# Two score products of 256 columns a head, with a query's two parts in the partition halves, in place of three of 512 a head pair

## The chip, the cores and the metric

The kernel runs on one core of a Trainium2 chip. The metric is the time of one execution on the device in microseconds. The core has five engines with a queue each: TensorE (PE in the profile; its weight loads are PEld), VectorE (DVE), ScalarE (ACT), GpSimd (POOL) and SyncE (SP), which issues the loads from memory. They work in parallel and wait for one another through semaphores.

## The reference

One decoder layer over 512 tokens of width 1024, all in 32-bit floats: a gated feed-forward half step (1024 to 2 x 2816 and back), a token mixer, a second feed-forward half step, and a gated embedding at the end. The mixer's attention is the part that is changed:

```python
s = jnp.einsum('bnqhgd,bnkhd->bnhgqk', qb, kb) * scale     # 16 query heads, 2 key heads, 64 wide
valid = (delta >= 0) & (delta < WINDOW) & (kpos >= 0)      # window of 128: this block and the one before
s = jnp.where(valid, s, NEG_INF)
m = jnp.maximum(jnp.max(s, -1, keepdims=True), sink)
pr = jnp.exp(s - m)
denom = jnp.sum(pr, -1, keepdims=True) + jnp.exp(sink - m)
o = jnp.einsum('bnhgqk,bnkhd->bnqhgd', pr / denom, vb)
```

Beside the attention the mixer has a branch with a causal convolution of 31 taps over 1024 channels and a layer norm, and two gates; the sum of both branches goes through one more matrix.

## The kernel before, in words

**Products in two parts.** Activations lie feature by token, in tiles of 128 features x 512 tokens. A 32-bit value is split into a high part, rounded to a shorter type that TensorE takes as it is (F32R), and a low part, the rest in the same type. ScalarE writes the high part, VectorE subtracts it from the value to get the low one (`split_into`). A product of two values is then three products on TensorE (`mm3`): low by high, high by high, high by low; low by low is left out. Every weight piece of 128 x 1024 is loaded, split and used so, through three buffers each for the raw piece, its high and its low part. In the list of weights, those of the mixer may be split on VectorE or on GpSimd (`FLEX`).

**The scores.** The 16 query heads lie in two groups g of eight, and the tokens in four blocks t of 128. `scores(g, t)` (L1083) takes four head pairs. Four transposes bring the queries of the block from token-major `zq` to `qTp`, in which a pair j stands with one head in partitions 0 to 63 and the other in 64 to 127. These two heads belong to the two different key heads. The keys `kz` (L1024) hold, for each key head, the 64 features in that head's half of the partitions and zeros in the other half; four memsets on GpSimd write the zeros. So a product of a pair's 128 partitions with the keys of both heads side by side gives each head's own scores: 2 x 256 columns where two key blocks are seen, 2 x 128 for t = 0, which sees one. With the three products of `mm3` that is 12 products for a call. ScalarE and VectorE then take the scores from PSUM under the mask, and VectorE takes maxima. `softmax` and `values` follow as separate steps.

**What sets the order.** The kernel is written as a list of operations, and a planner on the host puts them in order. The string `ORDER` (L40) names the steps of the mixer in the order in which TensorE should take them: K keys and values, Q queries, a and b the two projections of the convolution, A scores, E softmax, V values, g and h gates, p the attention's projection, L the norm of the convolution, e the embedding. `simulate` runs the list against costs from a table (`costs`, L291; a load is priced by its bytes over a rate, L344): each engine takes its ready operation with the earliest due time, TensorE takes groups of products from the next eight of the list, and operations of `nc.flex` go to whichever of VectorE and GpSimd comes first. Five rounds are made with due times from the round before, and the best one is kept. The program issues the operations in that order, and on the chip each engine keeps to it. So a new cost or a new step order moves operations on all engines.

**Names.** `q0b`, `q1b` are the query projections of the two groups, `kvb` that of keys and values, `ca`, `cb` those of the convolution, `ga`, `gb` gates, `ap` the attention's projection, `cp` the convolution's, `wo` the mixer's last one; `sc` scores, `pT` transposed probabilities and `p` their parts, `po` a masked copy of these, `o` values, `of` their sum, `oT` its parts; `cz` the running sum of a convolution channel in PSUM (VectorE, one operation a tap), `ct` taps of the channels that ScalarE and GpSimd do, `ln_` the convolution's norm, `cv` its result's parts, `e` and `ple` the embedding.

Of the kernel before, what the change touches and what calls it, by code (L numbers as in the profile page):

```python
# [9 lines left out]
F32 = mybir.dt.float32  # L10
F32R = mybir.dt.float32r
I32 = mybir.dt.int32
AF = mybir.ActivationFunctionType
# [3 lines left out]
P = 128  # L17
# [8 lines left out]
HD = 64  # L26
# [11 lines left out]


ORDER = """  # L40
K0 a0 a2 a1 Q0 A0 b2 b1 b0 a3 A1 E0 E1 b3 A2 E2 a4 V0 A3 a5 E3 V1 b4 Q1 V2 b5
A4 V3 A5 a7 A6 g5 h7 E5 A7 E6 E4 V6 g3 E7 g0 a6 V5 V4 g4 g6 b6 V7 h1 g2 h4 b7
g1 p0 p2 g7 L0 p3 p6 p4 h3 p7 p5 p1 e0 h5 h6 e1 h0 h2
"""
POOLCH = (0, 2, 4)
WARM = 9
# [178 lines left out]
class Program:  # L225
# [65 lines left out]
    def costs(self, op, eng=None):  # L291

        ins = op.reads
        o = op.writes[0] if op.writes else None
        n = max([v.free() for v in ([o] if o else []) + ins])
        psum = any(v.vt.cls == "ps" for v in op.writes + ins)
        eng = eng or op.eng
        op.lock = eng == "POOL"
        op.fset = None
        op.dma = 0.0  # L300
        vecs = sum(isinstance(v, V) for v in [*op.a[3:], *(v for n, v in op.k.items() if n != "accum_out")])
        if eng == "PE":
            if op.what == "transpose":
                op.cost, op.lat = 0.112, 0.3
            else:
                n = op.a[2].free()
                if op.a[2].vt.dtype == F32R:
                    op.cost, op.lat = (0.2275, 0.3) if n > 256 else (0.121, 0.3)
                else:
                    op.cost, op.lat = max(0.15, n * 0.00167), 0.35  # L310
        elif eng == "DVE":
            op.lat = 0.15
            if op.what == "tensor_tensor":
                op.cost = 0.065 + n * 1.055e-3
            elif op.what == "scalar_tensor_tensor":
                op.cost = 0.08 + n * 1.12e-3
            elif op.what == "tensor_tensor_reduce":
                op.cost = 0.28 + n * 1.02e-3
            elif op.what in ("reduce_sum", "tensor_reduce"):
                op.cost = 0.08 + n * 1.03e-3  # L320
            else:
                op.cost = 0.08 + n * (1.25e-3 if psum else 0.9e-3)
            op.lock = not psum and op.what not in ("tensor_tensor_reduce", "reduce_sum", "tensor_reduce", "reciprocal")
        elif op.what == "dma_start" and eng == "ACT":
            op.cost, op.lat = 0.5, 2.6
        elif eng == "ACT":
            op.cost, op.lat = 0.07 + n * 0.88e-3, 0.17
            op.cost += 0.094 * vecs
            if "accum_out" in op.k:
                op.cost += 0.1  # L330
            f = op.a[2].name if len(op.a) > 2 else "Copy"
            op.fset = SETS.get(f)
        elif eng == "POOL":
            op.lat = 0.15
            if op.what == "tensor_tensor":
                op.cost = 0.14 + n * 2.1e-3
            elif op.what == "tensor_scalar":
                op.cost = 0.25 + n * 0.8e-3
            else:
                op.cost = 0.12 + n * 1.0e-3  # L340
        else:
            op.cost, op.lat = 0.47, 0.0
            v = (op.writes + op.reads)[0]
            op.dma = v.free() * v.shape[0] * 4 / 360e3  # L344


class Engine:
# [296 lines left out]
def record():  # L644
# [8 lines left out]
    def rtile(name):  # L653
        return nc.tile(name, [P, S], F32R, "a")
# [367 lines left out]


    kz = [nc.tile(f"kz{p}", [P, NKV, S], F32R, "k") for p in "hl"]  # L1024
    for z in kz:
        nc.gpsimd.memset(z.bitcast(F32)[HD:P, 0], 0.0)
        nc.gpsimd.memset(z.bitcast(F32)[0:HD, 1], 0.0)


    vd = [nc.tile(f"v{t}", [P, 2, NKV, 2, HD], F32R, "a") for t in range(NT)]  # L1030
# [3 lines left out]
    def keys_values():  # L1034
# [26 lines left out]
        halves = [slice(hh * HD, (hh + 1) * HD) for hh in range(2)]  # L1061
        for hh in range(2):
            r = halves[hh]
            split_into(kz[0][r, hh], kz[1][r, hh], pt[r])

    zq, rq = {}, {}

# [15 lines left out]
    def scores(g, t):  # L1083
# [6 lines left out]
        with nc.group(f"qT{g}_{t}"):  # L1090
            for j in range(4):
                nc.tensor.transpose(pt[:, j * P : (j + 1) * P], zq[g, t][:, j * P : (j + 1) * P], ident)
        qT = split(f"qT{g}_{t}", pt)
        nb = 1 if t == 0 else 2
        t0 = t + 1 - nb
        s = [nc.tile(f"s{g}_{t}_{i}", [P, 2, 2, W], F32, "a") for i in range(2)]
# [1 line left out]
        for j in range(4):  # L1098
            ps = ps_tile(f"sc{g}_{t}_{j}")
            ps4 = ps.rearrange("p (h c k) -> p h c k", h=2, c=2)  # L1100
            with nc.group(f"sc{g}_{t}_{j}"):
                q = [qT[i][:, j * P : (j + 1) * P] for i in range(2)]
                kk = [kz[i][:, :, t0 * W : (t + 1) * W] for i in range(2)]
                mm3(ps4[:, :, 0:nb], q, kk, True, True)
            sj = s[j // 2][:, j % 2]
            if t == 0:
                nc.vector.tensor_tensor(sj, ps4[:, :, 0], later, op=ALU.add)
            else:
                nc.scalar.copy(sj, ps4[:, :, 1])
                nc.vector.copy_predicated(sj, later.bitcast(I32), ps4[:, :, 0])  # L1110
            if j % 2:
                mj = m[:, 2 * j - 2 : 2 * j + 2].rearrange("p (j h) -> p j h", h=2)
                nc.vector.tensor_reduce(mj, s[j // 2], axis=AX.X, op=ALU.max, negate=True)
# [332 lines left out]
```

## Time and profile before

| | |
|---|---|
| median of 3 runs | 1203.24 us (1203.09 to 1203.4) |
| the profiled execution, its span | 1205.14 us, 1203.4 us |
| TensorE busy | 1193.8 us, 99% |
| VectorE busy | 729.6 us, 61% |
| ScalarE busy | 506.7 us, 42% |
| GpSimd busy | 319.4 us, 27% |
| granted clock of TensorE | 0.999 |
| first feed-forward step, mixer, second step, embedding gate | to 369, to 803, to 1152, to 1203.4 us |

A time of a run is the device's; the span is that between the first and the last instruction of one execution that was taken with the profiler. A row of a group gives the line, the engine, the operation, out<-in with the shapes and the count, then busy time in us and the mean time of one in ns, then the idle time of the engine ahead of them. A row of the chain of waits or of the timeline gives start and length in us. A row of windows gives the stretch, its length, the busy time of an engine with its number of operations, the granted clock, the share of the DMA engines and GB/s. Nearly all operations are issued at one line of the kernel (L1346; L1354 in the changed file), so they are told apart by their tiles.

### The profile page before, as it was taken

The page shows a single profiled execution, that of the slowest core. Times are in us where ns is not written, and L with a number is a line of the kernel's source. Part 1 is how long each engine was busy: PE and PEld are TensorE (multiplying, and loading weights), DVE is VectorE, ACT ScalarE, POOL GpSimd, SP SyncE. Part 2 cuts the span into 40 slices and gives each one's busy share as a digit, 9 for nine tenths or more (in the row PEclk, how much of TensorE's full clock was granted, in tenths as well). Part 3 has the DMA queues.
Part 4 walks back from the last instruction along what each step waited for, and adds up shares of the span by engine and source line. Part 5 has one row for each costly group of instructions (what it writes and reads, how often), then busy time and mean ns, then how long its engine had stood idle before and what let it go on. Part 6 is the DMA issues. An engine that isn't in the chain of part 4 may idle for free.

```text
span 1203.4 us, 14206 instructions
## 1 busy us (share of the span) xinstructions
PE 1193.8 (99%) x5380; PEld 990.4 (82%) x5380; DVE 729.6 (61%) x1034; ACT 506.7 (42%) x821; POOL 319.4 (27%) x340
## 2 busy tenths in 40 slices
PE   9999999999999999999999999999999999999997
PEld 7888888888888888878888888888888888888886
DVE  5644444444444799998898786665444444444455
ACT  6423232332223669879854673323323332222232
POOL 1000000001111887887897500430000000011110
PEclk9999999999999999999999999999999999999999
DMA  7322223233332321212233222323232323333321
GB/s 222 105 92 100 96 98 100 88 114 97 97 101 88 105 88 53 89 53 71 76 101 101 92 88 89 104 88 105 88 105 88 105 90 99 96 97 96 101 88 71
DMA packets 36069, 115.06 MB, mean 96 GB/s; under 512 B 4512, under 2 KB 7200, under 8 KB 36000
## 3 DMA queue, kind: packets, MB, share of 16 engines
q1 hardware_dynamic: 35856, 114.12, 29.5%
q8 instruction: 42, 0.69, 0.2%
q14 instruction: 27, 0.22, 0.1%
q10 hardware_dynamic: 144, 0.03, 0.0%
HBM read 112.04 MB, written 2.10 MB: 95 GB/s over the span
## 4 chain that ended last, share of the span: by engine, by line
PE 96%; DVE 3%; issue 0%; ACT 0%; DMA 0%; POOL 0%; DVEq 0%; ACTq 0%; POOLq 0%
PE f_g L1346 20%; PE f_u L1346 20%; PE f_d L1346 20%; PE gb L1346 4%; PE cb L1346 4%; PE pg L1346 4%; PE wo L1346 4%; PE ap L1346 4%; PE cp L1346 4%; PE ca L1346 3%; PE ga L1346 3%; PE q0b L1346 2%; PE sc L1346 1%; DVE cz L1346 1%; PE kvb L1346 1%; PE e L1346 1%
## 5 line engine op out<-in xcount | busy, mean ns | idle before, releaser
L1346 ACT ACTIVATE whi_wgu<-raw_wgu 128x1024 fp32r<-128x1024 f32 (+1 forms) x100 | 95.1, 956 | 254.4 <-PE f_u L1346 231.1
L1346 DVE TENSOR_TENSOR wlo_wgu<-raw_wgu,whi_wgu 128x1024 fp32r<-128x1024 f32 (+1 forms) x100 | 110.8, 1112 | 112.0 <-ACT whi_wgu L1346 111.1
L1346 DVE TENSOR_TENSOR wlo_wd<-raw_wd,whi_wd 128x1024 fp32r<-128x1024 f32 (+1 forms) x48 | 65.8, 1370 | 101.9 <-ACT whi_wd L1346 101.9
L1346 ACT ACTIVATE whi_wd<-raw_wd 128x1024 fp32r<-128x1024 f32 (+1 forms) x48 | 47.5, 990 | 174.6 <-PE f_d L1346 113.1
L1346 POOL TENSOR_TENSOR y<-y,ct 128x509 f32<-128x509 f32 (+28 forms) x90 | 114.9, 1297 | 6.8 <-ACT ct L1346 5.1
L1346 DVE SCALAR_TENSOR_TENSOR cz<-u,dww,cz 128x504 f32<-128x504 f32 (+26 forms) x145 | 103.9, 731 | 1.7
L1346 POOL TENSOR_TENSOR pg_ss_sq<-x 128x512 f32<-128x512 f32 x8 | 8.3, 1041 | 338.1 <-DVE x L1346 324.1
L1346 POOL TENSOR_TENSOR mix_ss_sq<-x 128x512 f32<-128x512 f32 x8 | 8.3, 1041 | 328.3 <-DVE x L1346 316.3
L1346 DVE TENSOR_TENSOR f_gs<-f_g,f_n_rb 128x512 f32<-128x512 f32 x44 | 30.3, 691 | 94.4 <-PE f_g L1346 93.0
L1346 PE MATMUL f_d<-f_a_h,wlo_wd 128*128 128x512 f32 x224 | 87.1, 389 | 0.0
L1346 PE MATMUL f_d<-f_a_h,whi_wd 128*128 128x512 f32 x224 | 87.1, 389 | 0.0
L1346 PE MATMUL f_d<-f_a_l,whi_wd 128*128 128x512 f32 x224 | 87.1, 389 | 0.0
L1346 PE MATMUL f_g<-h_h,whi_wgu 128*128 128x512 f32 x176 | 69.1, 393 | 0.6 <-ACT whi_wgu L1346 0.6
L1346 PE MATMUL f_g<-h_h,wlo_wgu 128*128 128x512 f32 x176 | 69.2, 393 | 0.0
L1346 PE MATMUL f_g<-h_l,whi_wgu 128*128 128x512 f32 x176 | 69.0, 392 | 0.0
L1346 PE MATMUL f_u<-h_h,wlo_wgu 128*128 128x512 f32 x176 | 68.8, 391 | 0.0
L1346 PE MATMUL f_u<-h_l,whi_wgu 128*128 128x512 f32 x176 | 68.7, 390 | 0.0
L1346 PE MATMUL f_u<-h_h,whi_wgu 128*128 128x512 f32 x176 | 68.7, 390 | 0.0
L1346 PE MATMUL f_g<-f_h_h,wlo_wgu 128*128 128x512 f32 x176 | 68.6, 390 | 0.0
L1346 PE MATMUL f_g<-f_h_l,whi_wgu 128*128 128x512 f32 x176 | 68.5, 389 | 0.0
L1346 PE MATMUL f_u<-f_h_h,wlo_wgu 128*128 128x512 f32 x176 | 68.5, 389 | 0.0
L1346 PE MATMUL f_g<-f_h_h,whi_wgu 128*128 128x512 f32 x176 | 68.5, 389 | 0.0
(402 smaller groups left out, 3144.0 us busy)
## 6 DMA issues: line engine op xcount, KB each, us to landing
raw_wgu<-in_wgu SPq DMA_DIRECT2D x84, 512.0 KB, 3.5
raw_wd<-in_wd SPq DMA_DIRECT2D x32, 512.0 KB, 3.5
raw_wzc<-in_wzc SPq DMA_DIRECT2D x16, 512.0 KB, 3.4
raw_wzg<-in_wzg SPq DMA_DIRECT2D x16, 512.0 KB, 3.5
raw_wd<-in_wd SPq DMA_DIRECT2D x16, 384.0 KB, 3.1
raw_wq<-in_wq SPq DMA_DIRECT2D x8, 512.0 KB, 3.5
raw_wap<-in_wap SPq DMA_DIRECT2D x8, 512.0 KB, 3.5
raw_wcp<-in_wcp SPq DMA_DIRECT2D x8, 512.0 KB, 3.5
```

Source lines behind the costliest of these rows:

```text
L1346: getattr(engines[op.eng], op.what)(*a, **k)
```

## The change

The two parts of a query go into the two halves of the partitions. For each of the two heads of all pairs there is a tile `qT[hh]`: the high part stays in the half where the head came out of the transposes, and the low part is written into the other half. The keys of a head stand in both halves, in the high tile and in the low tile, so there are no zeros and no memsets. One product of `qT[hh]` with a key part then sums the high and the low query part against that key part; two products, with the low and with the high keys, make the scores of one head, low by low included. A call has 16 products, of 256 columns each, or of 128 for t = 0, where it had 12 of 512, or of 256. The splits are two on ScalarE and two on VectorE for a call, each on 64 partitions, where there was one of each on 128; for the keys there are four of each where there were two. With it come a new `ORDER`, and in the planner a load's rate of 240e3 in place of 360e3 bytes a microsecond.

```diff
 ORDER = """
-K0 a0 a2 a1 Q0 A0 b2 b1 b0 a3 A1 E0 E1 b3 A2 E2 a4 V0 A3 a5 E3 V1 b4 Q1 V2 b5
-A4 V3 A5 a7 A6 g5 h7 E5 A7 E6 E4 V6 g3 E7 g0 a6 V5 V4 g4 g6 b6 V7 h1 g2 h4 b7
-g1 p0 p2 g7 L0 p3 p6 p4 h3 p7 p5 p1 e0 h5 h6 e1 h0 h2
+K0 a0 a1 b1 Q0 b0 a2 b2 A0 a3 A1 b3 A2 E0 a4 V0 E1 A3 a5 E2 V1 b4 E3 Q1 V3 b5
+A4 g5 A5 a6 E4 A6 E5 V2 a7 b7 A7 g3 V5 b6 E6 h4 g4 V6 E7 g2 V4 V7 g6 g1 e0 g0
+p0 L0 p5 h2 h5 h3 h1 p6 p4 p3 p2 h6 e1 h7 h0 g7 p7 p1
 """
...
-            op.dma = v.free() * v.shape[0] * 4 / 360e3
+            op.dma = v.free() * v.shape[0] * 4 / 240e3
...
     kz = [nc.tile(f"kz{p}", [P, NKV, S], F32R, "k") for p in "hl"]
-    for z in kz:
-        nc.gpsimd.memset(z.bitcast(F32)[HD:P, 0], 0.0)
-        nc.gpsimd.memset(z.bitcast(F32)[0:HD, 1], 0.0)
...
             r = halves[hh]
-            split_into(kz[0][r, hh], kz[1][r, hh], pt[r])
+            for to in (r, halves[1 - hh]):
+                nc.scalar.activation(kz[0][to, hh], pt[r], AF.Copy)
+            for to in (r, halves[1 - hh]):
+                nc.vector.tensor_tensor(kz[1][to, hh], pt[r], kz[0][r, hh].bitcast(F32), op=ALU.subtract)
...
-        qT = split(f"qT{g}_{t}", pt)
+        qT = [rtile(f"qT{g}_{t}_{hh}") for hh in range(2)]
+        for hh in range(2):
+            r, other = (slice(h * HD, (h + 1) * HD) for h in (hh, 1 - hh))
+            nc.scalar.activation(qT[hh][r], pt[r], AF.Copy)
+            nc.vector.tensor_tensor(qT[hh][other], pt[r], qT[hh][r].bitcast(F32), op=ALU.subtract)
...
-                q = [qT[i][:, j * P : (j + 1) * P] for i in range(2)]
-                kk = [kz[i][:, :, t0 * W : (t + 1) * W] for i in range(2)]
-                mm3(ps4[:, :, 0:nb], q, kk, True, True)
+                for hh in range(2):
+                    for i in (1, 0):
+                        nc.tensor.matmul(
+                            ps[:, 2 * hh * W : (2 * hh + nb) * W], qT[hh][:, j * P : (j + 1) * P],
+                            kz[i][:, hh, t0 * W : (t + 1) * W], start=i == 1, stop=i == 0,
+                        )
```

The order moves as follows at three places. The first is TensorE at the first scores of the second query group (block t = 0). Before, from the transposes of the queries on (the 22 rows left out are the rest of the projection ca):

```order
L1346 MATMUL pT_3_0_4135<-ident,s_3_1_3728 128x128 x2
L1346 MATMUL qTp_0_4142<-ident,zq_0_4089 128x128 x4
L1346 MATMUL pT_3_1_4150<-ident,s_3_0_3697 128x128 x2
L1346 MATMUL pT_3_1_4150<-ident,s_3_1_3728 128x128 x2
L1346 MATMUL qTp_1_4160<-ident,zq_1_4096 128x128 x4
L1346 MATMUL ca_4170<-mix_h_h,wlo_wzc_4024 128x512
...
L1346 MATMUL sc_0_0_4228<-kzh,qT_0_l 128x2x128
L1346 MATMUL sc_0_0_4228<-kzh,qT_0_h 128x2x128
L1346 MATMUL sc_0_0_4228<-kzl,qT_0_h 128x2x128
```

The same place in the change:

```order
L1354 MATMUL qTp_0_4200<-ident,zq_0_4099 128x128 x4
L1354 MATMUL o_3_0_4208<-p_3_0_h,v_2773 128x512
L1354 MATMUL o_3_0_4208<-p_3_0_l,v_2773 128x512
L1354 MATMUL o_3_0_4208<-po_3_0h,v_2781 128x512
L1354 MATMUL o_3_0_4208<-po_3_0l,v_2781 128x512
L1354 MATMUL o_3_1_4219<-p_3_1_h,v_2773 128x512
L1354 MATMUL o_3_1_4219<-p_3_1_l,v_2773 128x512
L1354 MATMUL o_3_1_4219<-po_3_1h,v_2781 128x512
L1354 MATMUL o_3_1_4219<-po_3_1l,v_2781 128x512
L1354 MATMUL qTp_1_4229<-ident,zq_1_4108 128x128 x4
L1354 MATMUL sc_0_0_4239<-kzl,qT_0_0_4216 128x128
L1354 MATMUL sc_0_0_4239<-kzh,qT_0_0_4216 128x128
```

The projection ca no longer stands between the transposes and the scores; two groups of value products of the first head group do, and the transposes of the next block.

The second is VectorE at the same place, in the change. The operations qT are those that write the low query parts, of those that sum the values:

```order
L1354 TENSOR_TENSOR wlo_wzc_4183<-raw_wzc_4005,whi_wzc_4167 128x1024
L1354 SCALAR_TENSOR_TENSOR cz_3981<-u_3965,dww,cz_3981 128x500
L1354 SCALAR_TENSOR_TENSOR cz_3981<-u_3965,dww,cz_3981 128x499
L1354 TENSOR_TENSOR sga_4212<-ga_4140,mix_n_rb 128x512
L1354 SCALAR_TENSOR_TENSOR cz_3981<-u_3965,dww,cz_3981 128x498
L1354 TENSOR_TENSOR qT_0_0_4216<-qTp_0_4200,qT_0_0_4216 64x512
L1354 TENSOR_TENSOR qT_0_1_4224<-qTp_0_4200,qT_0_1_4224 64x512
L1354 TENSOR_TENSOR of_3_4231<-o_3_0_4208,of_3_4231 64x512
L1354 TENSOR_TENSOR of_3_4231<-o_3_1_4219,of_3_4231 64x512
L1354 TENSOR_TENSOR qT_1_0_4241<-qTp_1_4229,qT_1_0_4241 64x512
L1354 TENSOR_TENSOR qT_1_1_4249<-qTp_1_4229,qT_1_1_4249 64x512
```

Each block has two such operations where it had one, and they stand behind a weight split, tap operations and a gate of the projection ga.

The third is TensorE from the spread of the convolution norm's factors to the first convolution projection, in the change (rows left out are the rest of the two projections ap):

```order
L1354 MATMUL ln_v_sp<-ln_v_dgl,ones_r 128x512
L1354 MATMUL ap_6026<-oT0h,wlo_wap_5906 128x512
...
L1354 MATMUL ple_sp<-ple_dgh,ones_r 128x512
L1354 MATMUL ple_sp<-ple_dgl,ones_r 128x512
L1354 MATMUL ap_6078<-oT0h,wlo_wap_5943 128x512
...
L1354 MATMUL cp_6130<-cv_h,wlo_wcp_6036 128x512
```

Before, three quarters of the last embedding projection e and two gates gb stood there; now it is two projections ap.

## The prediction

> **What bounds the kernel now.** I read the page first, then TensorE's waits, then the windows by stage, then single groups.
>
> ```profile
> span 1203.4 us, 14206 instructions
> PE 1193.8 (99%) x5380; PEld 990.4 (82%) x5380; DVE 729.6 (61%) x1034; ACT 506.7 (42%) x821; POOL 319.4 (27%) x340
> PE 96%; DVE 3%; issue 0%; ACT 0%; DMA 0%; POOL 0%; DVEq 0%; ACTq 0%; POOLq 0%
> 249.34 119.68 PE f_d L1346 x528
> ```
>
> The first two rows are the page's head and its busy times, the third the chain that ended last by engine, the fourth one piece of that chain. TensorE is busy for all but 9.6 us of the span, and carries 96% of the chain. The fourth row gives the price that everything below uses: 528 products of 512 columns follow one another in 119.68 us, 0.2267 us from start to start (the 389 ns that the groups show for one is its latency, not its price). What else keeps the PE idle is little:
>
> ```profile
> PE warm L1346 <- DVE ones L1346: 1.1, 1, 1.1
> PE ca L1346 <- DVE of L1346: 1.1, 1, 1.1
> PE f_g L1346 <- ACT whi_wgu L1346: 0.6, 1, 0.6
> PE sc L1346 <- DVE of L1346: 0.3, 1, 0.3
> ```
>
> These four rows are all of its waits: 1.7 us at the start, which the change has no part in, and 1.4 us in the token mixer. So time is won only by giving TensorE less to do, and lost by making it wait. The engine that could make it wait is VectorE, in the stretch where the scores lie:
>
> ```profile
> 410.00:432.00 22.00, 20.83 (x25) 1.00 0.30 95
> 432.00:450.00 18.00, 17.93 (x42) 1.00 0.26 88
> 450.00:487.00 37.00, 35.13 (x67) 1.00 0.18 59
> 487.00:527.00 40.00, 38.71 (x61) 1.00 0.24 80
> 527.00:563.00 36.00, 33.72 (x67) 1.00 0.18 59
> 563.00:600.00 37.00, 31.75 (x46) 1.00 0.22 72
> 600.00:630.00 30.00, 28.54 (x40) 1.00 0.32 104
> 630.00:663.00 33.00, 28.02 (x38) 1.00 0.30 98
> ```
>
> Each row is a stretch, its length, and VectorE's busy time in it. From 410 to 663 us it is busy 234.6 of 253 us: 18.4 us are free, but only 4.4 of them before 527 us.
>
> **The scores of blocks t = 1 to 3.** Six of the eight calls have two key blocks.
>
> ```profile
> 442.73 1.43 PE sc L1346 x12
> 458.72 2.72 PE sc L1346 x12
> 369.02 11.51 PE kvb L1346 x96
> L1346 PE MATMUL sc<-kzh,qT_l 128*128 128x512 f32 x24 | 9.5, 397 | 0.3 <-DVE of L1346 0.3
> L1346 PE MATMUL kvb<-whi_wkv,mix_h_l 128*128 128x256 f32 x32 | 9.1, 283 | 0.0
> L1346 PEld LDWEIGHTS kvb<-whi_wkv,mix_h_l 128*128 128x128 f32 x32 | 6.1, 192 | 0.0
> ```
>
> Rows one to three are pieces of the chain: a t = 0 call, a later call, and the key and value projection. Now a later call is 12 products of 512, 2.72 us; 24 of each of three kinds, 72 x 0.2267 = 16.32 us. After the change it is 16 products of 256, 96 in all. That operation is in the trace: the key and value projection is 96 products of 256 columns, of the same type, each with a stationary tile of its own, in 11.51 us, 0.1199 each, although a weight load is shown as 192 ns; the loads overlap. So 96 x 0.1199 = 11.51 us, and this part saves 16.32 - 11.51 = **4.81 us**. The stationary tile now serves two products in a row; I count no gain for that, since two of each old triple share one too, and the t = 0 call still pays 1.43 / 12 = 0.119 for each.
>
> **The scores of block t = 0.** Two calls of 12 products of 256 columns, 2 x 1.43 = 2.86 us, become 32 products of 128 columns. The trace has no product of this type under 256 columns, so it is bounded.
>
> ```profile
> 467.21 1.03 PE L1346 MATMUL pT<-ident,s 128*128 128x128 f32 x8
> 468.00 0.47 PE L1346 MATMUL sc<-kzh,qT_l 128*128 128x512 f32 x1
> L1346 PE MATMUL warm<-ones 128*128 128x128 f32 x18 | 4.2, 430 | 1.1 <-DVE ones L1346 1.1
> 8.00 1.28 PE f_u L1346 x3
> ```
>
> The first two rows are single instructions in order of time, the third a group, the fourth a piece of the chain at the start. From below: 256 columns less cost 0.2267 - 0.1199 = 0.1068 us, so 128 less would cost 0.0534, leaving 0.0665 us each, 2.13 us, 0.73 less than now. From the nearest row: eight transposes of 128 columns, each with a new stationary tile, take from 467.21 to 468.00, 0.099 each: 32 x 0.099 = 3.17 us, 0.31 more than now. From above: the plain 32-bit warm-up products of 128 columns show 18 instructions for 9 calls in 4.2 us, 0.467 a call, at a time when three 512-column products took 1.28 us instead of 0.68; in the steady state that is 0.467 x 0.68 / 1.28 = 0.248 a call, and 32 x 0.248 = 7.94 us, 5.08 more than now. I take the transposes, as they have the same sizes: **+0.31**, from -0.73 to +5.08. This is the part in which narrower products speak against the change.
>
> By the Trainium skill (TensorE: Matmul & The Clock Gate, section LDWEIGHTS) a weight load takes its number of columns over 1.2, in ns, about 107 ns for 128 columns, whatever the matmul behind it. A product shorter than that would be held by its load, and the sum of this block would be 32 x 0.107 = 3.4 us, about 0.55 more than now. The 0.099 us of the transposes agrees to a tenth; no row here shows it for this type.
>
> **ScalarE and VectorE.** The operations change from one of 128 partitions to two of 64.
>
> ```profile
> L1346 ACT ACTIVATE kzh<-kTp x2: 577/588/598, 410.7 to 411.3; 64x512 fp32r<-64x512 f32 x2
> L1346 DVE TENSOR_TENSOR kzl<-kTp,kzh x2: 676/686/695, 411.9 to 412.6; 64x512 fp32r<-64x512 f32 x2
> L1346 ACT ACTIVATE qT_h<-qTp x8: 573/594/616, 437.8 to 541.2; 128x512 fp32r<-128x512 f32 x8
> L1346 DVE TENSOR_TENSOR qT_l<-qTp,qT_h x8: 676/683/692, 438.8 to 541.8; 128x512 fp32r<-128x512 f32 x8
> L1346 DVE TENSOR_TENSOR wlo_wgu<-raw_wgu,whi_wgu 128x1024 fp32r<-128x1024 f32 (+1 forms) x100 | 110.8, 1112 | 112.0 <-ACT whi_wgu L1346 111.1
> 487.00:527.00 40.00, 19.15 (x28) 1.00 0.24 80
> ```
>
> The first four are forms of one tile with their shortest, middle and longest time in ns; the fifth is a weight split; the last is the window from 487 to 527 us for the tap operations cz alone. Half the partitions cost the same (686 against 683 ns, 588 against 594). So eight query splits and two key splits more on each engine: VectorE gains 8 x 0.68 + 2 x 0.69 = 6.8 us, ScalarE 8 x 0.59 + 2 x 0.59 = 5.9 us. In the new order GpSimd also does two weight splits fewer (14, not 16), which VectorE then does at 1.11 us each: 9.0 us in all. GpSimd loses its four memsets, which lie at the start beside other work. ScalarE is at 42% and I price it at nothing beyond the chain below. VectorE's 9.0 us fit into its 18.4 free ones; the cover is the long row of tap operations cz, which nobody waits for before the norm of the convolution. Without that cover it would be those 9.0 us.
>
> **Where the new order is narrow.** At the first call of the second head group the old order had a whole projection (24 products, 5.44 us) between the transposes qTp_0 and the products. The new one has two value groups and four transposes: 8 x 0.2267 + 4 x 0.099 = 2.2 us. In that time ScalarE must do two halves and VectorE two, of which the last sub must follow the last copy: 0.59 + 0.59 + 0.68 = 1.9 us and the handovers between. Behind the two halves on VectorE stand the subtractions of_3 that free the value banks, so a late one there is late twice. I charge 0.5 us, up to 3 if VectorE comes to it late. On the other side the old stall (PE ca, 1.1 us, and sc, 0.3) stood just where this order is rewritten: after the query projection q1b there now stands a whole ga projection before the next transposes. It may go: -1.4.
>
> The second place is the convolution's norm.
>
> ```profile
> 688.09 0.39 PE L1346 MATMUL ln_v_sp<-ln_v_dgl,ones_r 128*128 128x512 f32 x1
> 689.18 0.60 ACT L1346 COPY ln_v_rb<-ln_v_sp 128x512 f32<-128x512 f32 x1
> 690.97 1.28 ACT L1346 ACT_TABLE_LOAD   x1
> 700.48 0.81 ACT L1346 ACTIVATE y<-y,g_all 128x512 f32<-128x512 f32 x1
> 701.70 0.82 ACT L1346 ACTIVATE y<-y,g_all 128x512 f32<-128x512 f32 x1
> 704.23 0.39 PE L1346 MATMUL cp<-cv_h,wlo_wcp 128*128 128x512 f32 x1
> ```
>
> Now cp follows ln_v_sp by 16 us; in the new order two ap projections and ple_sp lie between, 2 x 5.44 + 0.45 = 11.3 us. ScalarE needs from ln_v_sp 1.3 us to the end of the copy, 0.5 for a gate, 1.28 for the table, 8 x 1.22 (the step from one y to the next, 700.48 to 701.70), 1.5 for a copy and a weight split put in between; VectorE's last sub adds 0.7: 15.1 us. The eighth channel is wanted at 11.3 + 7 x 0.68 = 16.1. It holds by 1 us, and I charge nothing. Over both places and the old stall I take **+0.3**, from -1.4 to +3.
>
> The planner's dearer DMAs move some small loads and two splits of p ahead; weights still come through three buffers that TensorE frees, so I price it at zero, within 0.3 either way.
>
> **The sum.** -4.81 + 0.31 + 0.3 = -4.2 us. The profiled execution took 1205.14 us around its span of 1203.4; it becomes 1200.9, and the median of the runs shown, 1203.24, becomes **1199.0**. With the bounds of the likeliest case (t = 0 at 0.0665 to 0.12 a product, stalls -1.4 to +1.5) it lies from 1196.3 to 1200.9.
>
> **Rivals.**
>
> *Under 256 columns this type falls back to the price of the plain one.* Then t = 0 costs +5.08, and the time is 1203.24 - 4.81 + 5.08 + 0.3 = 1203.8. For it: the warm-up rows show that the plain type pays double instructions. Against it: nothing here shows the type switching. The Trainium skill (FP8 and Floating Point Precision, section TensorE Precision Notes) says that true FP32 takes four passes through the array; by that t = 0 would cost about four times its columns, much like the rows' bound.
>
> *New waits eat most of it*: 3 us at the two narrow places, 1203.24 - 4.81 + 0.31 + 3 = 1201.7. For it: VectorE has 1.3 us free from 487 to 527. Against it: 19.15 of its 38.71 us there are cz, which can wait.
>
> *VectorE becomes the bound (slower).* If its free time is not free but the waiting of an ordered queue, its added 9.0 us come out at ln_mb, which waits for the last cz, and everything behind it is late by 9.0 us less what can be filled. With a third of the 18.4 us filled, 9.0 - 6.1 = 2.9 us: 1206.1. It means slower than before by over 0.2% from the point at which less than 6.6 us can be filled. Against it: TensorE waits for VectorE 1.4 us today with VectorE 97% busy, and in the new order the work that stands ahead of ln_mb on TensorE is, by the prices above, 1.4 us more than now.
>
> *The change gives nothing because loads bind*: at 188 to 192 ns a load, 128 products would take 24 us instead of 19.2: 1208. The key and value row above all but excludes it.
>
> **Chances.** Likeliest 62%, fall-back to the plain price 14%, new waits 14%, VectorE the bound 8%, loads 2%. The runs tell a change from none at about 0.2%, 2.4 us, so 1200.8 and 1205.6 are the borders. The likeliest case lies under 1200.8 almost whole, and a little of the waits with it: faster 0.64. The fall-back and nearly all of the waits lie between: same 0.27. Slower 0.09. The range reaches from 1196.8 over the waits to the fall-back, 1204.
>
> **What would show it.** The sc groups: x48 of 256 columns for each key part, and a later call's piece of the chain at 1.92 us instead of 2.72; a t = 0 call at 1.6 (right), 1.1 (lower bound) or 4 (fall-back). VectorE's busy time near 738.6 us. TensorE's waits should still sum to about 3 to 4 us; a wait of sc or o on VectorE at the second head group, or of cp on cv, is the second rival, and one of ln_mb on ln_s_l the third. A wrong price of 256 columns, or stalls that grow by over 2 us, would make the prediction wrong.

## The result and the profile after

| | before | after |
|---|---|---|
| median of 5 runs | 1203.36 us (1203.09 to 1205.06) | 1211.07 us (1210.1 to 1215.47) |
| ratio to before, 95% interval | | 1.0063 (1.0052 to 1.0073) |
| the profiled execution, its span | 1205.14 us, 1203.4 us | 1211.07 us, 1209.4 us |

The change was to save 4.2 us and costs 7.7 by the medians. Executions of one kernel start in two ways, about 1.6 us apart in their time (windows at the last experiment show it); the two profiled ones compared here both start the later way, and differ by 5.9 us.

The first three rows are the page's head, its busy times and the chain by engine; the others are TensorE's waits (what it waited for, us in total, times, longest).

```profile
span 1209.4 us, 14261 instructions
PE 1195.0 (99%) x5412; PEld 992.9 (82%) x5412; DVE 738.1 (61%) x1046; ACT 512.9 (42%) x831; POOL 319.0 (26%) x334
PE 95%; DVE 2%; ACT 1%; issue 1%; POOL 1%; DMA 0%; DVEq 0%; ACTq 0%; POOLq 0%
...
PE sc L1354 <- DVE qT L1354: 2.1, 4, 1.1
PE pT L1354 <- POOL s L1354: 1.9, 1, 1.9
PE o L1354 <- DVE s L1354: 1.4, 1, 1.4
...
PE cb L1354 <- DVE of L1354: 0.6, 1, 0.6
PE qTp L1354 <- DVE u L1354: 0.4, 1, 0.4
```

VectorE is 738.1 us busy, as the sum of its added operations said, and ScalarE is still at 42%. New are the waits. In the mixer they come to 6.8 us (with 0.2 each of kTp and of pT on VectorE), where they were 1.4: 5.4 more.

The products did what they should. One piece of the chain, and two rows of the timeline (start, length, the instruction):

```profile
531.96 1.92 PE sc L1354 x16
...
445.07 0.30 PE L1354 MATMUL sc<-kzl,qT 128*128 128x128 f32 x1 [0.38 <-DVE qT L1354]
...
446.54 0.28 PE L1354 MATMUL sc<-kzh,qT 128*128 128x128 f32 x1
```

A later call takes 1.92 us, 0.120 a product. In a call of block t = 0 the last two rows are 13 products apart, 0.113 each: 32 of them cost 3.62 us, 0.76 more than the old 2.86.

That leaves a part that no wait shows. These rows are windows: the stretch, its length, the busy time (and number) of TensorE, its weight loads, VectorE, ScalarE and GpSimd, then the granted clock of TensorE, the DMA share and GB/s.

```profile
443.00:447.00 4.00, 2.38 (x17) 1.94 (x16) 3.85 (x8) 3.33 (x5) 3.92 (x4) 1.00 0.40 135
447.00:451.00 4.00, 3.81 (x12) 3.23 (x13) 3.97 (x8) 3.69 (x6) 3.57 (x3) 0.57 0.22 46
463.00:467.00 4.00, 2.10 (x18) 1.89 (x18) 3.98 (x10) 3.98 (x13) 2.66 (x6) 1.00 0.00 0
467.00:471.00 4.00, 4.00 (x13) 3.22 (x13) 3.90 (x8) 3.94 (x14) 0.95 (x3) 0.57 0.37 133
689.00:692.00 3.00, 3.00 (x27) 2.88 (x26) 0.86 (x2) 1.58 (x2) 1.16 (x1) 1.00 0.37 141
692.00:697.00 5.00, 5.00 (x17) 3.95 (x17) 4.61 (x32) 0.34 (x2) 1.21 (x1) 0.66 0.34 105
448.53 0.63 PE L1354 MATMUL cb<-mix_h_h,whi_wzc 128*128 128x512 f32 x1
...
450.24 0.48 PE L1354 MATMUL cb<-mix_h_l,whi_wzc 128*128 128x512 f32 x1
```

Behind a stretch in which TensorE was half idle (2.38 and 2.10 of 4 us), and behind 24 products of one column in a row (689 to 692), its clock falls for about 3.4 us. In that time 512-column products follow one another by 0.43 us, not 0.2267: the last two rows, of the timeline, are four products apart. The time lost is what the clock withheld: 4 x 0.43 + 4 x 0.43 + 5 x 0.34 = 5.1 us. In the kernel before the 16 one-column products ln_v_cs stand alone, ahead of products at full clock; the new order puts the 8 of ple_cs right behind them.

So the account is -4.81 + 0.76 for the products, 5.4 for waits, 5.1 for the clock: 6.5 us, against 6.0 between the spans. It says where the time went, and not yet why the waits came.

Where the first wait comes from is seen on three engines in the timeline of after, ScalarE (ACT), VectorE (DVE) and TensorE:

```profile
436.55 2.01 DVE L1354 TENSOR_TENSOR wlo_wzc<-raw_wzc,whi_wzc 128x1024 fp32r<-128x1024 f32 x1
...
442.23 0.63 ACT L1354 ACTIVATE sg<-sg 128x512 f32<-128x512 f32 x1 [3.39 <-DVE sg L1354]
442.89 0.59 ACT L1354 ACTIVATE qT<-qTp 64x512 fp32r<-64x512 f32 x1
443.51 1.41 DVE L1354 TENSOR_TENSOR qT<-qTp,qT 64x512 fp32r<-64x512 f32 x2
444.25 0.33 PE L1354 MATMUL sc<-kzl,qT 128*128 128x128 f32 x1 [1.06 <-DVE qT L1354]
```

The second query half on ScalarE (442.89) stands in its queue behind the gate `sg`, for which ScalarE idles 3.39 us. That gate waits for VectorE, which has no gap: a weight split of 2.01 us, taps cz, then sg. VectorE's subtractions follow the late half, and TensorE waits for them.

### The profile page after: what moved, and what is told of

It reads as the page before. It is cut to its first block, busy times and chain, and to the rows that moved or that the text cites. A ratio compares the mean times of both kernels' runs of the same rounds, so it can differ in the third digit from the quotient of the medians.

```text
span 1209.4 us, 14261 instructions
## 1 busy us (share of the span) xinstructions
PE 1195.0 (99%) x5412; PEld 992.9 (82%) x5412; DVE 738.1 (61%) x1046; ACT 512.9 (42%) x831; POOL 319.0 (26%) x334
## 4 chain that ended last, share of the span: by engine, by line
PE 95%; DVE 2%; ACT 1%; issue 1%; POOL 1%; DMA 0%; DVEq 0%; ACTq 0%; POOLq 0%
PE f_g L1354 20%; PE f_u L1354 20%; PE f_d L1354 20%; PE ga L1354 4%; PE pg L1354 4%; PE cp L1354 4%; PE gb L1354 4%; PE wo L1354 4%; PE ap L1354 4%; PE ca L1354 3%; PE cb L1354 2%; PE q0b L1354 2%; PE q1b L1354 2%; PE kvb L1354 1%; PE e L1354 1%; PE o L1354 1%
## 5 line engine op out<-in xcount | busy, mean ns | idle before, releaser
L1354 POOL TENSOR_TENSOR y<-y,ct 128x491 f32<-128x491 f32 (+29 forms) x90 | 120.2, 1356 | 9.9 <-ACT ct L1354 8.1
L1354 DVE SCALAR_TENSOR_TENSOR cz<-u,dww,cz 128x507 f32<-128x507 f32 (+25 forms) x145 | 103.5, 731 | 1.6
```

The lines of the kernel that those rows point to most:

```text
L1354: getattr(engines[op.eng], op.what)(*a, **k)
```

## The experiments

The diffs are shortened: switches that choose between the kernels, and the code that keeps a plan, are left out.

Theories in words. **Order**: the new step order (with the new load rate) is at fault. **Plan**: any new plan costs as much as this one. **Queue**: the added halves find no free time on VectorE and ScalarE where the scores lie, and TensorE, sooner with its products, only meets their queues. **Chain**: two halves lengthen the way from a block's transposes to its products, however free the engines are. **Clock**: part of the loss is the granted clock. The expectations call some of them by other names: A is the order, D the plan, B the halves making TensorE wait (the chain, whatever the order), C VectorE's part of the queue, PACE ScalarE's part of it, A2 narrow products that upset the order.

**Old order with the changed scores.** The planner makes a new plan from the old steps.

```diff
-K0 a0 a1 b1 Q0 b0 a2 b2 A0 a3 A1 b3 A2 E0 a4 V0 E1 A3 a5 E2 V1 b4 E3 Q1 V3 b5
+K0 a0 a2 a1 Q0 A0 b2 b1 b0 a3 A1 E0 E1 b3 A2 E2 a4 V0 A3 a5 E3 V1 b4 Q1 V2 b5
 ... (the whole of ORDER, and the rate back to 360e3)
```

> Only the products, the query splits and the key splits of the change; the step order and the load rate of before, so the planner orders the new list by the old rules. Theory A (the new step order and rate come late on the chip): TensorE saves about 4 us and the waits stay near before's, 1198 to 1201.5. Theory B (the second half-height split of each block on VectorE and ScalarE makes TensorE wait, in whatever order): 1205 to 1211.

Measured: 1211.54 us, 1.0059 (1.0041 to 1.0077). The same loss without the new order.

**New order with the old scores.** The reverse: only ORDER and the rate are the new ones. The diff is against the changed kernel.

```diff
-            for to in (r, halves[1 - hh]):
-                nc.scalar.activation(kz[0][to, hh], pt[r], AF.Copy)
 ...
+            split_into(kz[0][r, hh], kz[1][r, hh], pt[r])
 ... (queries, products and memsets as before)
```

> Only the new step order and load rate, with the three old products and the old splits. Theory A: the waits of the changed kernel are there without its products, and nothing is saved: 1206 to 1214. Theory B: no extra split, no extra wait: 1202 to 1205.

Measured: 1208.38 us, 1.0034 (1.0021 to 1.0047). So the new order has a price of its own with the old scores, with a wait of 1.8 us of sc on qT_l and a stretch of slow clock; but the two prices don't add up (0.59% and 0.34% alone, 0.63% together).

**The rate alone**, in the changed kernel:

```diff
-            op.dma = v.free() * v.shape[0] * 4 / 240e3
+            op.dma = v.free() * v.shape[0] * 4 / 360e3
```

> The changed kernel with the planner's load rate of before (360e3). If the rate makes the new order late: 1198 to 1202. If the step string or the splits do: 1207 to 1213.

Measured: 1211.55 us, 1.0061 (1.0046 to 1.0076): the rate makes nothing of the loss.

**The plan frozen.** Every operation keeps the place in its engine's queue, and the buffer, that it has in the kernel before; the scores' new products and splits are put where the old ones stood. The late half on ScalarE is put right ahead of VectorE's halves, up to some operations behind the early one.

```diff
-    prog = record()
+    prog = record(False)
 ...
-    return prog, spans[-1]
+    return thaw(prog), spans[-1]   # the changed program in the plan of the old one
```

> Before's own order, instruction by instruction and buffer by buffer; only the score products and the splits are put in at the places of the old ones, with the second ScalarE half right ahead of the VectorE halves. Theory A: TensorE's saving of about 4 us shows, less up to 2 us where the second half comes late: 1199 to 1202. Theory B: the splits delay TensorE here as well, 1204 to 1210.

Measured: 1216.29 us, 1.0103 (1.0086 to 1.012), 13 us over before and above the range of either theory: with no order or plan changed the edit is dearer than in the change. The new order wins back about 5. TensorE's waits in that kernel begin so:

```profile
PE o L1417 <- ACT p_h L1417: 4.0, 1, 4.0
PE o L1417 <- DVE s L1417: 1.5, 1, 1.5
```

The longest is no wait for a query half. It is o, the product with the probabilities, and what is late is `p_h`, a copy on ScalarE. In all, the waits in the mixer come to 11.1 us there. The clock takes a further 5 us or so: it is 0.91 from 432 to 450 us, 0.90 from 470 to 487 and 0.91 from 527 to 545.

**The halves alone, and the products alone**, both in the frozen plan. For the first the queries are split in halves on each engine, and the key splits are made twice, but the products are those of before; for the second nothing is added to ScalarE and VectorE.

```diff
 # halves alone
+for hh in range(2):
+    nc.scalar.activation(qT[0][r], pt[r], AF.Copy)                       # 64 partitions each
+    nc.vector.tensor_tensor(qT[1][r], pt[r], qT[0][r], op=ALU.subtract)
 # products alone
+split_into(qT[0], qT[1], pt)                                             # one of 128 partitions each
+for hh in range(2):
+    for i in (1, 0): nc.tensor.matmul(ps[...], qT[hh][:, j], kz[i][:, hh, ...])   # 256 columns
```

> Before's frozen order and its three old products; only each query split is done in two halves of 64 partitions on ScalarE and on VectorE (and the key splits twice), at the places of e4. Nothing is gained on TensorE. Theory B (the extra halves make TensorE wait): 1208 to 1217, that is e4 plus what the products save. Theory A2 (the halves are harmless, the narrow products upset the order): 1203 to 1205.

> Before's frozen order and its whole 128-partition splits; only the products are the new ones (16 a call, 256 or 128 columns). It leaves out the writing of the query parts and keys into both halves, so the scores are those of one query part. Theory B: TensorE's saving shows, 1198.5 to 1200.5. Theory C (VectorE sets the pace of this stretch, so that products are worth nothing): 1202 to 1204.5. Theory A2: 1206 to 1215.

Measured: the halves alone 1215.03 us, 1.0089 (1.0071 to 1.0107); the products alone 1205.13, 1.0002 (0.9992 to 1.0012). The halves, put at these places, are nearly the whole loss, and the 4 us of the products are worth nothing by themselves. Other places for the late half were not tried, so how much of this is the work and how much its place in the queue is not shown. The waits of the products alone:

```profile
PE o L1432 <- ACT p_h L1432: 1.4, 1, 1.4
...
PE ca L1432 <- DVE of L1432: 1.0, 1, 1.0
PE o L1432 <- DVE p_l L1432: 0.9, 2, 0.6
...
PE sc L1432 <- DVE of L1432: 0.7, 1, 0.7
```

With one more of 0.2 these are 4.2 us, 2.8 more than before. The window of this kernel from 450 to 487 us has the rest:

```profile
450.00:487.00 37.00, 35.36 (x185) 30.18 (x184) 34.14 (x63) 36.09 (x99) 27.28 (x42) 0.95 0.17 58
```

The clock is at 0.95, 37 x 0.05 = 1.9 us. What TensorE no longer spends on products it spends on waiting and on the slow clock that follows the wait.

**A new plan without any other edit**: the kernel before with the rate of the change, which moves some instructions on all engines.

```diff
-            op.dma = v.free() * v.shape[0] * 4 / 360e3
+            op.dma = v.free() * v.shape[0] * 4 / 240e3
```

> Before with only the planner's load rate at 240e3: same products, splits and step string, another order of the instructions. Theory D (before's order is a lucky one, and any new plan costs several us): 1206 to 1211. Theory B: within 2 us of before, 1202 to 1205.

Measured: 1203.35 us, 0.9995 (0.9986 to 1.0005). This new plan costs nothing, so the theory that any new plan costs as much falls.

**One-column products in a row**, in the kernel before: the column sums ln_v_cs are made three times, 48 products for 16.

```diff
-            for t in range(NT):
+            for t in list(range(NT)) * 3:
```

> Before's frozen order, with the column sums of the convolution's norm done three times (48 one-column instructions in place of 16, each time overwritten with the same sums). They cost 32 x 0.0985 = 3.15 us. If a stretch of one-column products brings the slow clock, another 1.7 us comes on top and the window behind it shows a granted clock near 0.6: 1207.5 to 1209. If not: 1206 to 1207, less what was waiting time before.

Measured: 1210.87 us, 1.0054 (1.0038 to 1.007), 6.2 us over before and above the range of both cases, where the 32 added products are worth some 3.2 by their own steps. The windows have the rest:

```profile
679.00:684.00 5.00, 5.00 (x31) 5.00 (x30) 1.11 (x1) 0.32 (x1) 0.00 (x0) 0.62 0.30 105
684.00:690.00 6.00, 6.00 (x18) 4.99 (x18) 3.80 (x17) 0.20 (x1) 0.00 (x0) 0.50 0.01 3
690.00:695.00 5.00, 5.00 (x22) 4.08 (x21) 1.15 (x2) 1.55 (x3) 0.00 (x0) 0.96 0.00 0
```

From 684 to 690 us TensorE is busy throughout at a clock of 0.50, 6 x 0.50 = 3.0 us lost, and its waits are those of the kernel before. So a long row of one-column products alone brings the slow clock.

**VectorE relieved.** Every second tap of cz is left out in the kernel before (the control) and in the frozen change.

```diff
+            if ext and THIN and d > 2 and d % 2:
+                continue                       # 14 of 31 taps of five channels
```

> Before's frozen order, old products and splits, but the five convolution channels of VectorE leave out every second tap from the third on (14 operations a channel, 70 in all, some 46 us of VectorE). The control for the next run. If VectorE is what TensorE waits for in this stretch, its 1.4 us of waits go: 1201.5 to 1203 where before gives 1203 to 1205.

> The same taps left out, with the products and splits of the change at before's frozen places (e4 with a relieved VectorE). Theory C (VectorE sets the pace; its queue is what turns the saving into waits): TensorE's saving of 4 us shows against the control, 1197.5 to 1200. If the length of each block's own chain (copy, copy, subtract, subtract) is what costs, VectorE's relief changes little: 1208 to 1216.

Measured: the control 1200.84 us, 0.9975 (0.9965 to 0.9985), without a wait in the mixer; the change 1208.31, 1.0034 (1.0021 to 1.0046), 7.5 over its control (about 6.2 with like starts). VectorE's lack of time is a part of the loss, and not all.

**The halves doubled on one engine only**, no taps left out.

```diff
 # on VectorE only: one copy of 128 partitions on ScalarE, two subtractions of 64 on VectorE
 # on ScalarE only: two copies of 64 partitions on ScalarE, one subtraction of 128 on VectorE
```

> Before's frozen order and old products; the query and key splits are doubled on VectorE alone (two halves), ScalarE does its one whole copy. Theory C: most of e5's 10 to 12 us, 1210 to 1215. If ScalarE's queue carries it: 1203 to 1206.

> Before's frozen order and old products; the splits are doubled on ScalarE alone, VectorE subtracts once, whole. Theory C: 1203 to 1207. If ScalarE's queue carries it: 1209 to 1215.

Measured: VectorE only 1209.48 us, 1.0042 (1.0027 to 1.0057); ScalarE only 1208.79, 1.0035 (1.0022 to 1.0048). With like starts VectorE's ten added operations (6.8 us by the prediction's own count) cost 5.3 us, ScalarE's (5.9 us) cost 3.9, and both together, in the run of the halves alone, 11.7, of which some 1.7 is slow clock (0.90 from 470 to 487 us). So neither engine alone carries the loss, and only a fifth to a third of the added time is hidden. TensorE's waits in the mixer, 1.4 us before, are 5.2 with VectorE doubled, the longest 1.7 us of o on the masked scores s, and 3.9 with ScalarE doubled, the longest 1.3 of o on p_h.

**Why there is no room on ScalarE** is seen in the kernel before, in windows of which the prediction shows only VectorE's column. The third row is the changed kernel:

```profile
450.00:487.00 37.00, 37.00 (x178) 30.24 (x177) 35.13 (x67) 36.60 (x103) 29.05 (x43) 1.00 0.18 59
...
527.00:563.00 36.00, 36.00 (x168) 29.85 (x168) 33.72 (x67) 33.65 (x92) 29.71 (x38) 1.00 0.18 59
...
450.00:487.00 37.00, 34.30 (x177) 28.91 (x176) 34.20 (x70) 32.33 (x93) 25.84 (x38) 0.95 0.17 58
```

Before, ScalarE is busy 36.60 of 37 us from 450 to 487 us, and VectorE 35.13; from 527 to 563 us, where the second head group's softmax lies, both 33.7 of 36. In the change ScalarE is busy only 32.33 of the same 37 us: there it isn't full but waits in its order, as at the gate sg above.

Two ways lead through this stretch of the old plan, and the timelines show both ends; for TensorE, which does not wait for whi_wzc, its start is only a common mark. ScalarE's first instruction is the weight copy whi_wzc, for which it sat idle 3.65 us; behind it, in order and without a gap, come the score copies, the softmax's exponentials and at last p_h. TensorE does two projections and the score calls in the same time, and then needs p_h for o. Before, the products alone, the ScalarE halves, and the frozen change with VectorE relieved:

```profile
450.17 1.07 ACT L1346 ACTIVATE whi_wzc<-raw_wzc 128x1024 fp32r<-128x1024 f32 x1 [3.65 <-POOL y L1346]
...
468.30 1.10 ACT L1346 ACTIVATE p_h<-pT 128x512 fp32r<-128x512 f32 x2
469.47 0.40 PE L1346 MATMUL o<-p_h,v 128*128 128x512 f32 x1
```

```profile
450.11 1.07 ACT L1432 ACTIVATE whi_wzc<-raw_wzc 128x1024 fp32r<-128x1024 f32 x1 [3.66 <-POOL y L1432]
...
468.23 1.09 ACT L1432 ACTIVATE p_h<-pT 128x512 fp32r<-128x512 f32 x2
468.89 0.50 PE L1432 MATMUL o<-p_h,v 128*128 128x512 f32 x1 [1.39 <-ACT p_h L1432]
```

```profile
450.26 1.06 ACT L1440 ACTIVATE whi_wzc<-raw_wzc 128x1024 fp32r<-128x1024 f32 x1 [3.16 <-POOL y L1440]
...
470.36 1.08 ACT L1440 ACTIVATE p_h<-pT 128x512 fp32r<-128x512 f32 x2
471.01 0.50 PE L1440 MATMUL o<-p_h,v 128*128 128x512 f32 x1 [1.28 <-ACT p_h L1440]
```

```profile
449.00 1.06 ACT L1440 ACTIVATE whi_wzc<-raw_wzc 128x1024 fp32r<-128x1024 f32 x1 [2.89 <-issue]
...
469.37 1.09 ACT L1440 ACTIVATE p_h<-pT 128x512 fp32r<-128x512 f32 x2
470.02 0.69 PE L1440 MATMUL o<-p_h,v 128*128 128x512 f32 x1 [3.23 <-ACT p_h L1440]
```

ScalarE's way from whi_wzc to p_h takes 18.13 us before and 18.12 with the products alone: it does not care for the products. TensorE's way to o, without its wait, falls from 19.30 (469.47 - 450.17) to 17.39 (468.89 - 1.39 - 450.11). It had 0.5 us in hand, since o can follow p_h by 0.66 and followed by 1.17; of the 1.91 saved, 1.39 becomes a wait. With two halves more on ScalarE (18.13 to 20.10) its way is 1.97 us longer, almost 1 us a half, where one lasts 0.59; the rest is lost at handovers, since neighbours in the queue overlap by some 0.1 us and those next to a late half don't. In the frozen change with VectorE relieved, 20.37, both meet: o waits 3.23.

**Both engines relieved.** The taps on ScalarE and GpSimd are thinned too; control, change, and products alone.

```diff
-            if ext and THIN and d > 2 and d % 2:
+            if THIN and d > 2 and d % 2:       # all eight channels
```

> This control is the kernel before in its own order, with every second tap of the convolution from the third on left out for all eight channels (so the convolution and what follows it is not the reference's): 14 VectorE instructions less for each of five channels, as in the run that thinned VectorE, and now also 14 ScalarE products (ct) and 14 GpSimd additions less for each of the other three. By 42 times the 701 ns of the ct group ScalarE gets 29 us less to do, and GpSimd 42 times 1.30 = 54 us less. TensorE had no wait left in the mixer when VectorE alone was thinned (1200.84 us), so by both theories this is 1200 to 1201 us.

> The same thinning of both engines with the changed scores and splits put into the order of before. Theory QUEUE (the halves cost because VectorE's and ScalarE's queues have no free time where the scores lie, ScalarE 36.6 of 37 us): with free time on both, the waits of o on p_h and s shrink below 1 us and the time falls under the control, by 3 to 4.5 us (the 4.81 saved on the products, less the dearer block t = 0): 1196.3 to 1198. Theory CHAIN (the two halves lengthen the way from the transposes to the products and the order has no room for that, however free the engines are): the waits stay in sc and o, and it is 4 us or more above the control, as it was 7.5 above with VectorE alone thinned.

> The same thinning of both engines with the products alone: each query part is split whole, in one operation an engine, and the scores are those of one query part only (not the reference's), with 16 products of 256 columns a call. Both theories: nothing is added to the two engines, so the products' saving comes out in full, 3.5 to 4.5 us under the control (1196.3 to 1197.5), where the same edit was worth nothing beside busy queues (1205.13 against 1204.65). If it stays within 1 us of the control, the products are not cheaper in time at all and the price of 256 columns was wrong.

Measured: 1201.74, 1209.18 and 1201.80 us; ratios to before 0.9979 (0.997 to 0.9988), 1.0046 (1.0031 to 1.0061), 0.998 (0.997 to 0.9989). By the words of the expectations the chain won: the change is 7.4 over its control, and the products are worth nothing. But the relief had missed its place. In the control ScalarE is still busy for 36.25 of the 37 us from 450 to 487, since only two of the four taps that it has there were left out:

```profile
450.00:487.00 37.00, 37.00 (x180) 30.61 (x179) 29.48 (x58) 36.25 (x103) 23.41 (x38) 1.00 0.18 57
L1440 ACT ACTIVATE s<-s,m,q_r 128x128 f32<-128x128 f32 x29 | 14.1, 493 | 0.1
L1440 ACT ACTIVATION_READ_ACCUMULATOR s<-s,m,q_r 128x1 f32 x29 | 5.7, 197 | 0.0
```

The window and two groups of that control: what fills ScalarE most there is the softmax. Its exponentials and the reads of their sums are 19.8 us long in all; as they overlap, one pair follows the other by 0.48 us, so they take some 14 of the 37 us.

**The softmax itself made shorter**, on top of it.

```diff
-        nc.gpsimd.tensor_tensor(es, sinks[...], m, op=ALU.add)
+        nc.gpsimd.tensor_tensor(es, sinks[...], sinks[...], op=ALU.subtract)
 ...
-            nc.scalar.activation(si, si, AF.Exp, bias=m[:, v], scale=rq[g][t][:, v], accum_out=den[:, v])
+            sx = si[:, 0:16] if t else si
+            nc.scalar.activation(sx, sx, AF.Exp, bias=m[:, v], scale=rq[g][t][:, v], accum_out=den[:, v])
```

> Control. The thinned kernel before (both engines' taps), and in addition the 48 exponentials of the blocks t = 1 to 3 work on the first 16 of their 128 keys, and the sink's term is taken as exp(0), so the attention and what follows it is not the reference's. Thinning the taps left ScalarE 36.25 of 37 us busy from 450 to 487 us, because what fills it there is the softmax (29 exponentials at 493 ns with 29 accumulator reads at 197 ns). An exponential of 8 columns (es) takes 209 ns, so one of 16 should take about 230 ns, 0.26 us less: 28 of them free about 7 us in that stretch. TensorE had no wait there in the control before this one: 1201 to 1202 us, as that (1201.74).

> The same relief with the changed scores and splits. Theory PACE (from 450 to 487 us the softmax on ScalarE sets the pace, and the added halves lengthen that queue): with 7 us free there, the wait of o on p_h (3.2 us) goes, and the time comes within 2 us of its control or under it, 1198 to 1203. Theory CHAIN (the halves lengthen the way from a block's transposes to its products, whatever the queues hold): the waits of o and sc stay near 6 us in sum and it stays 5 us or more above the control, as it was 7.4 above with the taps thinned.

> The same relief with the products alone (scores of one query part, not the reference's; no added halves). Theory PACE: TensorE can now run ahead, the waits of o on p_h go, and the products' saving comes out: 3 to 4.5 us under the control. Theory CHAIN: the products were worth nothing beside the taps thinned (1201.80 against 1201.74) because the way from scores through softmax to o is a chain that is no shorter when TensorE is sooner; a shorter exponential shortens that chain too, so the saving comes out here as well. This run tells whether the 4.8 us exist at all: if it is within 1 us of the control, the price of 256 columns or something else that no theory names is wrong.

Measured: the control 1201.80 us, 0.998 (0.9971 to 0.999); the change 1205.60, 1.0011 (1.0002 to 1.0021); the products alone 1199.30, 0.9961 (0.9946 to 0.9976). Eight times fewer columns made an exponential only 95 ns shorter, 399 for 493, not 260: the relief is 48 x 0.095 = 4.6 us and ScalarE is still busy for 35.18 of 37. Even so the change went from 7.4 over its control to 3.8 (with like starts from 7.9 to 4.4), and the products alone from nothing to 2.5 under it. Of that last number a part is the start: their four runs lie at 1198.4 to 1198.5 and 1200.1 to 1200.2, the control's ten at 1200.2 to 1200.6 and 1201.4 to 1202.2; like against like it is 1.9. The profiled executions, in the windows from 5 to 10 us, the control first:

```profile
5.00:10.00 5.00, 3.85 (x16) 2.76 (x16) 3.73 (x8) 4.29 (x11) 0.00 (x0) 1.00 1.03 342
```

```profile
5.00:10.00 5.00, 4.13 (x10) 2.75 (x10) 3.74 (x8) 4.36 (x11) 0.00 (x0) 1.00 1.03 325
```

With 4.6 us taken from ScalarE's softmax, wherever it lies, the products' saving begins to come out, and the change loses nearly half of its loss. That is what a full queue does; as the expectation of the last run says, a chain that is made shorter does it as well, so these runs don't tell the two apart. Nor was the expected size met: the change was to be within 2 us of its control, and o still waits 2.84 us for p_h. ScalarE's rows of the change with short exponentials show why:

```profile
468.62 0.40 ACT L1442 ACTIVATE s<-s,m,q_r 128x16 f32<-128x16 f32 x1 [1.09 <-DVE m L1442]
...
470.11 1.08 ACT L1442 ACTIVATE p_h<-pT 128x512 fp32r<-128x512 f32 x2
470.75 0.80 PE L1442 MATMUL o<-p_h,v 128*128 128x512 f32 x1 [2.84 <-ACT p_h L1442]
```

Here ScalarE has time and idles 1.09 us, for the maxima m of the next block, which come from its scores, which came late from the halves; and p_h stands behind that exponential in the queue. So the chain has a share too, through the order of a queue. About 5 of the 13 us of the frozen change are the slow clock that follows the waits; how the waits divide between full queues and chains through them isn't settled: no run has a ScalarE that is really free there.

## Why the prediction was wrong

It said 1199.0 us and faster; it is 1211.07 and slower, above the range as well.

- *"ScalarE is at 42% and I price it at nothing beyond the chain"* is the step that failed. 42% is a mean over the whole span. Where the scores lie it is 36.60 of 37 us, in the same windows of which the prediction reads VectorE's column. Its ten operations alone cost about 4 us.
- *"VectorE's 9.0 us fit into its 18.4 free ones"* failed as well. Ten halves on VectorE alone cost about 5 us. The third rival's reason, that free time in a window is the waiting of an ordered queue, is what the timeline of after bears out: the taps cz were to give way, but they stand in a fixed order ahead of the gate sg and don't.
- *The stalls, +0.3, at most +3*: they were +5.4. That they grew by over 2 us is the sign of being wrong that the prediction names. The two places I named are no worse than I said: at the second head group the products wait 0.24 and 0.38 us, and cp does not wait. The stalls came elsewhere: at the first head group's first call, at pT (1.9) and at an o (1.4).
- *The products, -4.81*: right as a price, 0.120 each. As time it came out only in part and only where ScalarE was relieved (1.9 us); in the plan of before it is worth nothing by itself.
- *Block t = 0, +0.31*: it measured +0.76. The transposes were the right row to go by (0.113 for 0.099, far from both bounds), a term mis-sized. By the Trainium skill (TensorE: Matmul & The Clock Gate, section LDWEIGHTS) a load of 128 columns takes about 0.107 us. The prediction's estimate from it, 3.4 us for the block, was nearer to the 3.62 measured.
- *The granted clock* was no term at all, and took 5.1 us, by two stalls and by a step order that puts two rows of one-column products together.
- *The third rival, VectorE the bound*, had the right sign for the wrong place: nothing waits at ln_mb. That its time, 1206.1, lies on the right side of before is luck in part: it has no term for the clock. No rival had ScalarE in it.
- *The rate, zero*: right, in both kernels. VectorE's busy time, 738.6: 738.1.

## What to carry to other kernels

Before time is priced as hidden on an engine, read the busy time of **every** engine in the window where it will stand; a share of the whole span says nothing there. If two engines run side by side up to a point at which one needs the other, making one way shorter gains only until the other is the longer, so find the point at which they meet (here o and p_h) and measure both ways to it before cutting either. A copy split into two halves of the partitions cost its whole time twice here (0.59 us each), and on an engine with an ordered queue that lands on whatever stands behind it.

## What the runs showed of the hardware

- A stall of about 2 us in 4, or 24 to 48 one-column products in a row, brought TensorE's clock to about half for some 3.4 us (0.57 in 4 us, 0.50 in 6), with 512-column products 0.43 us apart; 16 in a row, before, did not. Nor did each such stall: with ScalarE only doubled TensorE is busy 2.23 of 4 us, and the clock stays at 1.00 (rows below, TensorE alone). What decides is not shown. The Trainium skill (TensorE: Matmul & The Clock Gate, Part 1) tells of a clock that halves after an idle window of about 3.4 us and needs as long to come back. The length and the half agree with these rows. That the window must be idle doesn't: it was half idle here, and with the one-column products the profile shows TensorE busy throughout.

```profile
468.00:472.00 4.00, 2.23 (x11) 1.00 0.00 0
472.00:476.00 4.00, 3.98 (x20) 1.00 0.01 4
```

- An exponential with a sum on ScalarE lasts 399 ns for 16 columns and 493 for 128, and the read of its sum 197 more; as they overlap, one pair follows the other by 0.38 and 0.48 us. An eighth of the columns saves a fifth of the time.
- Half the partitions are no cheaper: a query copy of 64 partitions takes 0.59 us on ScalarE, as one of 128 did, and each added one lengthened its way by almost 1 us.
